# A convolution and SwiGLU layer on one core: the sixteen dot products of the first norm's gate move from the start of the second input stage to the end of the first

## The chip, the core and the metric

The kernel runs on one core of a Trainium2 chip. A core has TensorE (PE, matrix products into PSUM), VectorE (DVE), ScalarE (ACT), GpSimd (POOL) and SyncE (SP), which here only issues transfers. Each engine works off its own list of instructions in order and waits for the others by semaphores. The metric is the device time of one execution in microseconds; lower is better.

## What is computed

With DEPTH 1 the reference is one layer over 2048 tokens of 1024 features, float32, batch 1:

```python
c_act = jax.nn.silu(c)
mod = c_act @ ada_w[0] + ada_b[0]
sh_m, sc_m, g_m, sh_f, sc_f, g_f = jnp.split(mod, 6, axis=-1)
h = modulate(rms_norm(x, norm_gains[0, 0]), sh_m, sc_m)
h = short_conv_mixer(h, conv_w_in, conv_w, conv_w_out)   # 1024 -> 3072, gate_c * v,
                                                         # 3 taps, gate_b, 1024 -> 1024
x = x + g_m * rms_norm(h, norm_gains[0, 1])
h = modulate(rms_norm(x, norm_gains[0, 2]), sh_f, sc_f)
h = swiglu(h, w_gate_up, w_down)                         # 1024 -> 2 x 2816 -> 1024
x = x + g_f * rms_norm(h, norm_gains[0, 3])
```

The change is about `g_m`, the third of the six vectors of 1024 numbers that come from the conditioning vector `c`. In the kernel it is number 2 (numbered from 0). It is the gate by which the normalised result of the convolution mixer is scaled before it is added to `x`.

## The kernel before

**Stages.** The tokens are worked on in two units of 1024, each unit in two halves of 512 tokens. Every unit passes four stages of matrix products: `in` (the input projection with the convolution behind it), `out` (the output projection), `gu` (gate and up) and `down`. Their order is in0, out0, in1, out1, gu0, down0, gu1, down1. Tiles carry the stage's name: `in1P` is a block of PSUM in the second input stage.

**Products.** Each 2 x 2 product of blocks is made with seven products, P1 to P7, instead of eight, from sums and differences of blocks of the features (A11, A12, A22, S1 to S4) and of the weights. To keep float32 accuracy each operand is split into a high and a low part (`...h` and `...l`), and three matmuls stand for one product. One slot is one such product for one group of output columns: four blocks of 128 features, 12 matmuls of 128x512. The whole program is one list of slots, and slot numbers are the clock of the code: `first["in1"]` is the number of the slot with which in1 begins. in0 has 84 slots, out0 has 36, in1 has 84; the first two of out0 stand ahead of the last two of in0, so `first["out0"]` is 82 and `first["in1"]` is 120.

**Order.** For each slot the code first prepares weights for later slots (`supply`: load, sum, split into high and low), then does what was scheduled for this slot, then the small generators that are due (`due`), then the matmuls (`multiply`) and what follows on them. All engines keep the order in which the code issues, so an instruction that is issued early and waits holds up what stands behind it on the same engine. `schedule(slot, f)` runs `f` at a slot; a generator that yields a number goes on that many slots later.

**The modulation vectors.** Vectors 0 and 1 are made at the very start. The others, one each, are made by `mods_later(ms, pace)`: for each half of `c` it loads the row of `c`, spread over all partitions, applies Silu on ACT, and then makes eight dot products on VectorE (`tensor_tensor_reduce`, in the trace CUSTOM_DVE_ANT_0 with a short DVE_READ_ACCUMULATOR2_ANT behind it), each over a tile of 128 rows by 512 columns of `ada`, that is 16 for a vector. Each tile of `ada` is loaded by SP three steps ahead of its product. After the 16 products three small operations form the result, for vector 2 `mG[0]`. Between two steps lie `pace` slots. Vector 3 is scheduled at `first["out0"] - 2`, vector 4 at `first["in1"] + 60`, vector 5 in down0.

**Who uses it.** `mG[0]` is read by `after_out`, which starts when a half of `out0` is done and begins its own scaling about 40 slots later, inside in1.

**Tiles that are shared.** The tiles of `ada` and of the row of `c` come from the pool `raw`: 16 tiles of 128x512. From the same pool come the weight blocks of the input stage (`in10b`), the weights for the sums of the output stage (`out3b`), the rows of `x` for the next unit's norm (`xr`), the output stage's weights, and in in0 one of the PSUM copies of each group (`self.c22`, made by ACT). A load whose tile is not free yet waits on SP, and all of SP's later loads and stores wait behind it. Split weights use a pool of seven pairs (`wp`).

**Around the places.** In the last slots of in0 run the last weight sums for the output stage (`sums_later("out", ...)` from slot 24, on POOL and SP) and the norm of the next unit's rows (`norm_of_rows`, from slots 51 and 77, on ACT and SP). At the beginning of in1 `normalized` prepares the features of the new unit: it scales the loaded tiles a to d on VectorE, shifts them on ACT, and makes the seven operands (`s1`, `s3`, `s4`, `upper`, `lower`, `high`, `low`). In1's first groups read their weights from DRAM, where in0 left them (`in5P2k` is such a load).

Of the kernel before, what the change touches and what calls it, by code (L numbers as in the profile page):

```python
# [49 lines left out]
def hybrid_conv_layer(  # L50
# [43 lines left out]
    def raw(name):  # L94
        return raws.tile([P, CH], F32, tag="raw", bufs=NRAW, name=name)
# [7 lines left out]
    def small(n, name):  # L103
        return sb.tile([P, n], F32, tag="small", bufs=16, name=name)
# [8 lines left out]
    def later(slots, f):  # L113
        waiting.append((now[0] + slots, len(waiting), f))

    def run(gen):


        def step():
            n = next(gen, None)  # L120
            if n is not None:
                later(n, step)

        step()
# [38 lines left out]
    def col(t, k):  # L163
        return t[:, k : k + 1]
# [8 lines left out]
    def mods_later(ms, pace):  # L173

        s2 = {(m, h): sb.tile([P, KD], F32, tag="ms", bufs=4, name=f"ms{m}_{h}") for m in ms for h in range(2)}
        for h in range(2):
            half = slice(h * CH, (h + 1) * CH)
            row = raw(f"c{ms[0]}_{h}")
            SP.dma_start(row, c_row[:, half].to_broadcast((P, CH)))
            todo = [(m, n) for m in ms for n in range(KD)]  # L180
            tiles = {}

            def load(i, half=half, todo=todo, tiles=tiles):
                if i < len(todo):
                    m, n = todo[i]
                    tiles[i] = raw(f"ada{m}_{half.start}_{n}")
                    SP.dma_start(tiles[i], ada[m - 1, n][:, half])

            load(0)
            yield pace  # L190
            load(1)
            yield pace
            A.activation(row, row, AF.Silu)
            load(2)
            yield pace
            for i, (m, n) in enumerate(todo):
                load(i + 3)
                t = tiles.pop(i)
                V.tensor_tensor_reduce(t, t, row, 1.0, 0.0, ALU.mult, ALU.add, col(s2[m, h], n))
                yield pace  # L200
        for m in ms:
            i, which = m // 3, m % 3
            t = small(KD, f"mf{m}")
            V.tensor_tensor(t, s2[m, 0], s2[m, 1], ALU.add)
            b = vt[:, VB + m * KD : VB + (m + 1) * KD]
            if which == 0:
                V.tensor_tensor(mB[i], t, b, ALU.add)
            else:
                V.tensor_tensor(t, t, b, ALU.add)
                g = VG + (2 * i + which - 1) * KD  # L210
                if which == 1:
                    V.scalar_tensor_tensor(mA[i], t, 1.0, vt[:, g : g + KD], ALU.add, ALU.mult)
                else:
                    V.tensor_tensor(mG[i], t, vt[:, g : g + KD], ALU.mult)
            yield 1
# [650 lines left out]
    slots, first, own = [], {}, {}  # L866
# [13 lines left out]
    def schedule(slot, f):  # L880
        events.setdefault(max(slot, 0), []).append(f)
# [503 lines left out]
    schedule(24, lambda: run(sums_later("out", range(4), 2)))  # L1385
    schedule(first["gu0"] + 64, lambda: run(sums_later("down", range(12), 1.1)))
    schedule(first["out0"] - 2, lambda: run(mods_later((3,), 1.25)))
    schedule(first["in1"] - 8, lambda: run(mods_later((2,), 1.25)))
    schedule(first["in1"] + 60, lambda: run(mods_later((4,), 1.25)))
    schedule(first["down0"] + 22, lambda: run(mods_later((5,), 2)))  # L1390
    schedule(first["down1"] + 73, lambda: before_last(phases[-1]))
# [92 lines left out]
```

## Time and profile before

| | |
|---|---|
| median of 3 runs | 1970.31 us (1970.17 to 1972.41) |
| the profiled execution | 1969.02 us |
| its span, from first to last instruction | 1967.2 us |
| busy: PE, DVE, ACT, POOL | 1939.6, 1464.8, 870.2, 342.4 us |
| transferred | 459.51 MB, mean 234 GB/s |
| granted TensorE clock | 1.000 of full speed |

All durations below come from the profiled execution. In a timeline row stand the start, the length, the engine, the line of the code (always L78, the helper through which all instructions pass), the operation, the tiles as out<-in, the shape, the count and, in brackets, how long the engine was idle before it and whose signal came last. In a list of waits stand the total, how often, and the longest. SPq is SP's queue of transfers. Where a wait for several signals ended, the name given is the one that came last by the profile, which need not be the one that mattered.

### The profile page before, as it was taken

The page shows a single profiled execution, that of the slowest core. Times are in us where ns is not written, and L with a number is a line of the kernel's source. Part 1 is how long each engine was busy: PE and PEld are TensorE (multiplying, and loading weights), DVE is VectorE, ACT ScalarE, POOL GpSimd, SP SyncE. Part 2 cuts the span into 40 slices and gives each one's busy share as a digit, 9 for nine tenths or more (in the row PEclk, how much of TensorE's full clock was granted, in tenths as well). Part 3 has the DMA queues.
Part 4 walks back from the last instruction along what each step waited for, and adds up shares of the span by engine and source line. Part 5 has one row for each costly group of instructions (what it writes and reads, how often), then busy time and mean ns, then how long its engine had stood idle before and what let it go on. Part 6 is the DMA issues. An engine that isn't in the chain of part 4 may idle for free.

```text
span 1967.2 us, 24986 instructions
## 1 busy us (share of the span) xinstructions
PE 1939.6 (99%) x8468; PEld 1571.7 (80%) x8468; DVE 1464.8 (74%) x2159; ACT 870.2 (44%) x1430; POOL 342.4 (17%) x224
## 2 busy tenths in 40 slices
PE   8899999999999999999999999999999999999998
PEld 4578887777888888888888888888888888888886
DVE  5998888988998876997776755586776655665466
ACT  4533447534335643444333454463333333444452
POOL 0012202201221301243341410120100100111010
PEclk9999999999999999999999999999999999999999
DMA  9369859869996764677665977577554342386534
GB/s 390 137 230 390 306 178 350 314 236 373 327 319 228 265 228 146 223 240 249 212 211 189 307 292 264 181 278 270 195 194 136 126 142 97 118 312 232 196 133 133
DMA packets 204752, 459.51 MB, mean 234 GB/s; under 512 B 22864, under 2 KB 38352, under 8 KB 198224
## 3 DMA queue, kind: packets, MB, share of 16 engines
q1 hardware_dynamic: 180000, 403.52, 59.4%
q10 hardware_dynamic: 24624, 54.40, 7.2%
q8 instruction: 66, 1.08, 0.2%
q14 instruction: 62, 0.51, 0.1%
HBM read 326.75 MB, written 131.07 MB: 233 GB/s over the span
## 4 chain that ended last, share of the span: by engine, by line
PE 88%; DVE 5%; DMA 3%; issue 2%; ACT 1%; SPq 0%; POOL 0%; ACTq 0%; POOLq 0%; DVEq 0%
PE gu0P L78 21%; PE gu1P L78 21%; PE in0P L78 11%; PE down0P L78 11%; PE down1P L78 9%; PE in1P L78 8%; PE out1P L78 4%; PE out0P L78 2%; DVE in1c L78 0%; DVE ada L78 0%; DMA in0a<-xt_d 0%; DMA c<-c_row_d 0%; DMA y1S<-in1b1s 0%; DVE in1y L78 0%; PE pms L78 0%
## 5 line engine op out<-in xcount | busy, mean ns | idle before, releaser
L78 DVE TENSOR_TENSOR gu1a<-gu1P,gu1a 128x512 f32<-128x512 f32 x63 | 43.5, 691 | 108.6 <-PE gu1P L78 108.6
L78 DVE TENSOR_TENSOR gu0a<-gu0P,gu0a 128x512 f32<-128x512 f32 x63 | 43.3, 688 | 70.2 <-PE gu0P L78 68.6
L78 POOL TENSOR_TENSOR gu1a<-gu1a 128x512 f32<-128x512 f32 x11 | 19.0, 1726 | 363.5 <-DVE gu1g11s L78 42.5
L78 ACT COPY gu1a<-gu1P 128x512 f32<-128x512 f32 x42 | 24.7, 587 | 98.6 <-PE gu1P L78 87.4
L78 POOL TENSOR_TENSOR nq<-nq,nq 128x512 f32<-128x512 f32 x28 | 41.6, 1485 | 129.4 <-ACT nq L78 99.4
L78 ACT COPY gu0a<-gu0P 128x512 f32<-128x512 f32 x42 | 24.4, 586 | 83.8 <-PE gu0P L78 82.7
L78 DVE CUSTOM_DVE_ANT_0 ada<-ada,c 128x512 f32<-128x512 f32 x80 | 57.8, 733 | 0.0
L78 ACT COPY gu1g<-gu1P 128x512 f32<-128x512 f32 x24 | 14.1, 588 | 92.9 <-PE gu1P L78 92.9
L78 POOL TENSOR_TENSOR gu0a<-gu0a 128x512 f32<-128x512 f32 x11 | 19.4, 1767 | 171.4 <-ACT gu0a L78 48.0
L78 POOL TENSOR_TENSOR down0q<-down0q,down0q 128x512 f32<-128x512 f32 x14 | 23.8, 1703 | 144.1 <-ACT down0q L78 144.1
L78 ACT COPY gu0g<-gu0P 128x512 f32<-128x512 f32 x24 | 14.1, 587 | 75.9 <-PE gu0P L78 75.4
L78 POOL TENSOR_TENSOR down1q<-down1q,down1q 128x512 f32<-128x512 f32 x10 | 16.1, 1612 | 148.6 <-ACT down1q L78 148.6
L78 DVE TENSOR_TENSOR gu1g<-gu1P,gu1g 128x512 f32<-128x512 f32 x24 | 16.6, 691 | 27.4 <-ACT gu1g L78 26.0
L78 ACT ACTIVATE gu1a<-gu1a 128x512 f32<-128x512 f32 x42 | 26.6, 633 | 13.2 <-DVE xo L78 6.0
L78 DVE TENSOR_TENSOR down2P<-down2P,down2P 128x512 fp32r<-128x512 f32 x14 | 11.1, 794 | 28.6 <-ACT down2P L78 28.6
L78 ACT ACTIVATE gu0a<-gu0a 128x512 f32<-128x512 f32 x42 | 26.6, 633 | 11.7 <-DVE gu0a L78 10.4
L78 POOL TENSOR_TENSOR out1q<-out1q,out1q 128x512 f32<-128x512 f32 x14 | 22.3, 1594 | 51.2 <-ACT out1q L78 51.1
L78 POOL TENSOR_TENSOR out0q<-out0q,out0q 128x512 f32<-128x512 f32 x14 | 23.0, 1641 | 44.6 <-ACT out0q L78 44.5
L78 DVE TENSOR_TENSOR xx<-xx,zz 128x512 f32<-128x512 f32 x32 | 27.1, 847 | 1.1
L78 ACT ACTIVATE nq<-xx 128x512 f32<-128x512 f32 x32 | 20.2, 631 | 17.3 <-DVE xx L78 17.3
L78 DVE TENSOR_TENSOR gu0g<-gu0P,gu0g 128x512 f32<-128x512 f32 x24 | 16.5, 689 | 14.7 <-ACT gu0g L78 13.3
L78 DVE TENSOR_TENSOR down10P<-down10P,down10P 128x384 fp32r<-128x384 f32 x14 | 8.6, 615 | 22.3 <-ACT down10P L78 22.3
(3225 smaller groups left out, 6729.3 us busy)
## 6 DMA issues: line engine op xcount, KB each, us to landing
ada<-ada_d SPq DMA_DIRECT2D x64, 256.0 KB, 5.6
act0A<-gu0a SPq DMA_DIRECT2D x33, 256.0 KB, 3.5
act1A<-gu1a SPq DMA_DIRECT2D x33, 256.0 KB, 2.8
ada<-ada_d SPq DMA_DIRECT2D x16, 512.0 KB, 9.4
zz<-z SPq DMA_DIRECT2D x32, 256.0 KB, 5.2
xx<-xt_d SPq DMA_DIRECT2D x32, 256.0 KB, 5.5
x<-xx ACTq DMA_DIRECT2D x32, 256.0 KB, 4.9
down0S<-act0S SPq DMA_DIRECT2D x8, 1024.0 KB, 7.1
```

The costliest lines, as they stand in the source:

```text
L78: return tc.keep_in_program_order(f(*args, **kwargs))
```

## The change

One line. The generator for vector 2 starts 23 slots before out0, that is at slot 59, with one slot between its steps; before, it started eight slots before in1, at slot 112, with 1.25 slots between them.

```diff
     schedule(first["out0"] - 2, lambda: run(mods_later((3,), 1.25)))
-    schedule(first["in1"] - 8, lambda: run(mods_later((2,), 1.25)))
+    schedule(first["out0"] - 23, lambda: run(mods_later((2,), 1.0)))
     schedule(first["in1"] + 60, lambda: run(mods_later((4,), 1.25)))
```

By the generator's steps (three, eight products, three, eight products) it takes 22 slots and then forms the result: slots 59 to 81 after the change, 112 to 139.5 before. It issues 18 loads on SP (two rows of `c`, sixteen tiles of `ada`), two Silu on ACT, and sixteen products and the three small operations on VectorE, the same in both kernels. Vector 3 keeps its slot 80, so it now follows vector 2 instead of going ahead of it.

## The prediction

> **What bounds the kernel now.** I read the page first (span, busy times, transfers), then the list of waits of TensorE by stretch, then the timelines of the engines around each wait, then the busy times by stretch.
>
> ```profile
> span 1967.2 us, 24986 instructions
> PE 1939.6 (99%) x8468; PEld 1571.7 (80%) x8468; DVE 1464.8 (74%) x2159; ACT 870.2 (44%) x1430; POOL 342.4 (17%) x224
> ada<-ada_d SPq DMA_DIRECT2D x64, 256.0 KB, 5.6
> ```
>
> TensorE is the bound: 99% busy. So the change can only win where TensorE waits, or lose by making it wait. The list of TensorE's waits has nothing between 466 and 1900 us. In the stretch that holds the beginning of the second input stage (360 to 466 us) it has this:
>
> ```profile
> PE in1P L78 <- ACT in1c L78: 2.1, 2, 1.2
> PE in1P L78 <- DVE n00q L78: 0.9, 1, 0.9
> PE in1P L78 <- DVE in1S2l L78: 0.6, 1, 0.6
> PE in1P L78 <- DVE in1C L78: 0.4, 1, 0.4
> PE in1P L78 <- DVE in1c L78: 0.2, 1, 0.2
> PE in1P L78 <- DMA in6P3k<-kin6P: 0.2, 1, 0.2
> ```
>
> That is 4.4 us of waiting, seven waits. Four of them stand in its timeline here (those on in1S2l, in1C and DVE's in1c lie between 374.71 and 397.89); the first two rows give TensorE's pace:
>
> ```profile
> 360.02 0.61 PE L78 MATMUL in1P<-in1A11h,in3P1k 128*128 128x512 f32 x2
> 362.74 0.61 PE L78 MATMUL in1P<-in1A11h,in4P1k 128*128 128x512 f32 x2
> ...
> 374.71 0.70 PE L78 MATMUL in1P<-in1A12h,in5P2k 128*128 128x512 f32 x2 [0.93 <-DVE n00q L78]
> 397.89 0.50 PE L78 MATMUL in1P<-in1S1h,in3P5k 128*128 128x512 f32 x1 [0.82 <-ACT in1c L78]
> 434.83 0.73 PE L78 MATMUL in1P<-in1S1h,in0P 128*128 128x512 f32 x2 [1.24 <-ACT in1c L78]
> 463.39 0.70 PE L78 MATMUL in1P<-in1S4h,in6P3k 128*128 128x512 f32 x2 [0.19 <-DMA in6P3k<-kin6P]
> ```
>
> A slot (12 matmuls) takes 362.74 - 360.02 = 2.72 us. Twelve slots lie between 360.02 and the product in1S1h,in3P5k. Without waiting it would begin at 360.02 + 32.6 = 392.7 (less than a microsecond later with a norm's eight one-column matmuls in between, which I leave out); it begins at 397.89. So up to 5.2 us are lost there, more than the waits listed (4.4 less those of 434.83 and 463.39, about 3), because the matmuls just after a wait run slow too.
>
> **What holds TensorE there.** VectorE works almost without a gap from 362 to 396 us, and the moved products stand in its row. Of its timeline and ACT's:
>
> ```profile
> 366.99 0.68 DVE L78 CUSTOM_DVE_ANT_0 ada<-ada,c 128x512 f32<-128x512 f32 x1
> 367.67 1.27 DVE L78 TENSOR_TENSOR out0z<-out0P,out0z 128x512 f32<-128x512 f32 x2
> 368.87 0.67 DVE L78 CUSTOM_DVE_ANT_0 ada<-ada,c 128x512 f32<-128x512 f32 x1
> 369.72 4.43 DVE L78 TENSOR_TENSOR in1e<-in1a,in1c 128x512 f32<-128x512 f32 x4 [0.17 <-ACT in1c L78]
> 375.74 0.68 DVE L78 CUSTOM_DVE_ANT_0 ada<-ada,c 128x512 f32<-128x512 f32 x1
> 381.42 2.28 DVE L78 TENSOR_TENSOR in1c<-in1c,in1d 128x2048 f32<-128x2048 f32 x1
> 389.05 0.68 DVE L78 CUSTOM_DVE_ANT_0 ada<-ada,c 128x512 f32<-128x512 f32 x1
> 389.65 1.29 DVE L78 TENSOR_TENSOR in1S2l<-in1a,in1S2h 128x512 fp32r<-128x512 f32 x2
> 393.13 2.28 DVE L78 TENSOR_TENSOR in1b<-in1b,in1a 128x2048 f32<-128x2048 f32 x1
> ...
> 368.98 2.55 ACT L78 ACTIVATE in1c<-in1c,mB 128x512 f32<-128x512 f32 x4
> 378.34 2.71 ACT L78 ACTIVATE in1d<-in1d,mB 128x512 f32<-128x512 f32 x4 [2.07 <-DVE in1d L78]
> 395.45 1.91 ACT L78 CAST in1S4h<-in1b 128x2048 fp32r<-128x2048 f32 x1 [5.66 <-DVE in1b L78]
> 397.26 0.58 ACT L78 COPY in1c<-in1P 128x512 f32<-128x512 f32 x1
> 433.67 0.62 ACT L78 CAST in0P<-in0b 128x512 fp32r<-128x512 f32 x1 [1.57 <-PE in1P L78]
> ```
>
> Read it from the end: TensorE waits at 397.89 for ACT's copy of in1P (397.26), which stands behind the cast in1S4h (395.45), which waited 5.66 us for VectorE's in1b (393.13). Ahead of that VectorE runs unbroken back to 369.72. One product takes 389.65 - 389.05 = 0.60 us of its time. Four stand between 369.72 and 393.13, the first at 375.74 and the last at 389.05.
>
> The first wait, at 374.71, is put down to n00q, but the weights in5P2k are what came last. Their load stood in SP's queue behind a moved load:
>
> ```profile
> 368.74 0.82 SPq L78 DMA_DIRECT2D ada<-ada_d  x1
> 369.67 0.37 SPq L78 DMA_DIRECT2D in5P2k<-kin5P  x1
> ```
>
> **The change part by part.** Removed from the second input stage: 16 products on VectorE (16 x 0.60 = 9.6 us), the small sums behind them, two Silu on ACT, 16 loads of ada and two of the c row on SP's queue. Up to 397.89:
>
> 1. The product at 366.99 goes, so out0z (367.67) comes 0.6 us earlier. ACT squares it before it shifts in1c (368.98), and in1e (369.72) waits for that shift. So in1e starts 0.6 us earlier. The product at 368.87 wins nothing: the 0.17 us of idle time shows that in1e waited for ACT.
> 2. The one at 375.74 goes: another 0.6, 1.2 so far. ACT's shift of in1d moves along with it.
> 3. The next one stands just ahead of in1c + in1d (381.42). That sum needs ACT's last shift, which ends at 378.34 + 2.71 = 381.05, so only about 0.3 of its 0.6 us is won: 1.5.
> 4. The other two (the last at 389.05) lie in an unbroken row: 1.2 more, 2.7 at in1b.
> 5. Cast and copy on ACT follow, and TensorE's product comes at 395.2 instead of 397.89. That is later than 392.7, so nothing else needs to be faster than now. The waits before it shrink or vanish inside this sum; in5P2k, needed at 374.71 - 0.93 = 373.8, leaves the queue at least 0.9 us earlier (369.67 - 368.74), with out0z's store ahead of it 0.6 earlier: 1.5 us, more than the wait.
>
> Gain there: 2.7 us. Bounds: 0.9 (only the wait for in5P2k goes, something not seen holds in1b) and 5.2 (all that is lost). I take 2.7, because each step has its row.
>
> After that: the wait of 1.24 us at 434.83 stays. The copy there stands behind the cast of 433.67, which waited for TensorE itself (for a weight buffer). The wait of 0.19 at 463.39 goes, 0.3 us with the slow matmul after it: VectorE is rid of the eight products of the second half as well, and the loads ahead of in6P3k follow its stores. Nobody else waits until 1900 us, so what is won stays: 2.7 + 0.3 = 3.0 us.
>
> Added, ahead of the first output stage. Slot first["out0"] is where out0P begins, at 273.62, and 23 slots earlier (23 x 2.72 = 62.6) is 211 us. By the code the 16 products come one a slot, with three slots of loads ahead of each half: they end by 274.
>
> ```profile
> 273.62 0.62 PE L78 MATMUL out0P<-out0A110h,out0P 128*128 128x512 f32 x2
> ...
> 126.00:211.00 85.00, 85.00 (x376) 70.36 (x375) 75.44 (x108) 31.31 (x56) 23.95 (x15) 1.00 0.99 374
> 211.00:274.00 63.00, 63.00 (x277) 51.79 (x277) 47.23 (x80) 25.76 (x52) 9.45 (x7) 1.00 0.68 230
> 337.00:443.00 106.00, 101.86 (x451) 82.55 (x450) 96.93 (x160) 50.18 (x79) 20.53 (x12) 1.00 0.79 276
> 443.00:466.00 23.00, 22.81 (x100) 18.22 (x98) 18.30 (x32) 10.12 (x18) 1.29 (x1) 1.00 1.02 363
> ```
>
> Columns of the last four rows: length, busy time of PE, PEld, DVE, ACT, POOL, granted clock, DMA share, GB/s. At the new place VectorE has 47.23 of 63 us; with 9.6 and the small sums it is 57.3, 91%. The 18 transfers of 256 KB are 4.7 MB, 75 GB/s more: 305. The stretch just before ran at 75.44 of 85 us (89%), a DMA share of 0.99 and 374 GB/s, and TensorE was busy 85.00 of 85.00. So I price the new place at 0, covered by VectorE's 15.8 us of idle time; if that cover fails, the price is the last rival's. SP's queue there gets the 18 issues, with w_in, w_out and x rows behind them; ACT, with 25.76 of 63 us, takes the two Silu. The gate is first read here, so an earlier result is not waited for and wins nothing:
>
> ```profile
> 458.93 0.75 DVE L78 SCALAR_TENSOR_TENSOR zz<-zz,mG,n00r 128x512 f32<-128x512 f32 x1
> ```
>
> **The sum.** The profiled execution took 1969.02 us, 1.8 beside its span; less 3.0 it is 1966.0. The median of the runs is 1.3 above it (1970.31), so I predict 1967.3.
>
> **The rivals.** *More is won.* The four in1e take 4.43 us where two such operations of the same size take 1.29 (389.65), so 2.6 undisturbed; they collide with POOL. If the shift by 0.6 us ends the collision, 1.8 us more come off the row, and the gain is 2.7 + 1.8 + 0.3 = 4.8 us, still within the 5.2: 1965.5. Against it: POOL's sums there are released through ACT by out0z, which moves as well. Chance 0.2.
> [...]
>
> *Nothing is won.* The DMA engines become the bound behind it: in6P3k lands when it lands now, and TensorE, 2.7 us ahead, waits 2.7 longer at 463.39. For it: the DMA share is 1.02 just there (443 to 466). Against it: the transfers ahead are stores of VectorE's results and loads into freed buffers, which move along. 1970.3, chance 0.17.
>
> *It is slower.* The tiles of the moved loads come out of the ring of 16 "raw" tiles that also serves the w_in blocks, the x rows, the sums for w_out and the copies of a product block. By the code five more are held in slots 62 to 66, and SP already waits there for tiles to come free:
>
> ```profile
> SPq L78 <- DMA kout2P<-out2b: 4.5, 3, 3.0
> ...
> 215.79 0.59 ACT L78 COPY in0b<-in0P 128x512 f32<-128x512 f32 x1 [3.46 <-PE in0P L78]
> 221.03 0.61 PE L78 MATMUL in0P<-in0S4h,in8P 128*128 128x512 f32 x2
> ```
>
> That copy takes such a tile, and in0S4h,in8P may begin only when it is done: 221.03 - 216.38 = 4.65 us of slack. If a tile comes three slots late (8.2 us), TensorE loses 3.5. Two such copies fall into the full slots: 7.0 less 3.0 is 4.0 slower, 1974.3. It decides from a delay of 4.65 + 1.5 = 6.2 us on both. Against it: VectorE's and ACT's release of tiles follows TensorE slot by slot, and I count a delay of one to two slots. Chance 0.11.
>
> **How the numbers follow.** The forecast has 0.52, with 1966.4 to 1969.1 as its own range (2.7 replaced by 3.6, halfway to the first rival, or by the bound of 0.9). The range reaches to the first two rivals: down to 1964.8 (the bound of 5.2 and the 0.3) and up to 1971.2 (nothing won, and a part of the slower case); it leaves out most of the slower case and a little of each end. Measurement tells about 0.2% (3.9 us) from no change. Faster by more than that: the rival that wins 4.8, 0.2, and a little of the forecast, 0.22. Slower: 0.11. Within: 0.67.
>
> **What would show it.** Right, if in the new profile: TensorE's wait at in5P2k is gone; in1b ends some 2.7 us earlier against the start of in1P; the wait on ACT in1c behind in1S4h is shorter but there; one wait of 1.2 us on ACT in1c remains in the product in1S1h,in0P; no wait of TensorE appears between 210 and 274 us, with VectorE near 91%. Wrong, if TensorE waits for ACT in0b or in0c there (the ring), if in6P3k is waited for by 2 us or more, or if in1e's four take under 3 us.

## The result

| | median | |
|---|---|---|
| before | 1971.13 us | 1968.90 to 1972.41, 16 runs |
| after | 1967.57 us | 1965.52 to 1969.67, 16 runs |
| after / before | 0.9981 | 95% interval 0.9975 to 0.9988 |

The change wins 3.6 us, 0.19%. The same kernel timed again beside the last experiments gave 1967.09 against 1970.43, a ratio of 0.9983 (0.9974 to 0.9991), 3.3 us. Predicted were 3.0 us and 1967.3. The profiled execution took 1968.11 us, only 0.9 less than the one before (1969.02); where the rest of the gain went in this execution is told below.

### The profile page after: what moved, and what is told of

It reads as the page before. It is cut to its first block, busy times and chain, and to the rows that moved or that the text cites. A ratio compares the mean times of both kernels' runs of the same rounds, so it can differ in the third digit from the quotient of the medians.

```text
span 1966.3 us, 24998 instructions
## 1 busy us (share of the span) xinstructions
PE 1939.7 (99%) x8468; PEld 1572.9 (80%) x8468; DVE 1463.6 (74%) x2159; ACT 870.3 (44%) x1430; POOL 343.1 (17%) x224
## 4 chain that ended last, share of the span: by engine, by line
PE 92%; DVE 3%; issue 2%; DMA 2%; ACT 1%; POOL 0%; ACTq 0%; POOLq 0%; SPq 0%; DVEq 0%
PE gu0P L78 21%; PE gu1P L78 21%; PE in0P L78 11%; PE down0P L78 11%; PE in1P L78 10%; PE down1P L78 9%; PE out1P L78 4%; PE out0P L78 3%; DMA x<-xx 0%; DMA in0a<-xt_d 0%; DMA c<-c_row_d 0%; PE pms L78 0%; DVE down1z L78 0%; DVE in1y L78 0%; DMA in7P2k<-kin7P 0%
## 5 line engine op out<-in xcount | busy, mean ns | idle before, releaser
L78 ACT COPY gu1a<-gu1P 128x512 f32<-128x512 f32 x42 | 24.7, 588 | 98.5 <-PE gu1P L78 87.4
```

The lines of the kernel that those rows point to most:

```text
L78: return tc.keep_in_program_order(f(*args, **kwargs))
```

## The profile after

The span, then the whole list of TensorE's waits from 360 to 1900 us (total, times, longest):

```profile
span 1966.3 us, 24998 instructions
```

```profile
PE in1P L78 <- ACT in1c L78: 2.3, 2, 1.4
PE in1P L78 <- DMA in7P2k<-kin7P: 0.4, 1, 0.4
```

Seven waits of 4.4 us before are three of 2.7 now. The timelines of TensorE, VectorE and ACT at the places that the prediction named:

```profile
361.49 0.61 PE L78 MATMUL in1P<-in1A11h,in3P1k 128*128 128x512 f32 x2
375.09 0.61 PE L78 MATMUL in1P<-in1A12h,in5P2k 128*128 128x512 f32 x2
396.62 0.73 PE L78 MATMUL in1P<-in1S1h,in3P5k 128*128 128x512 f32 x2 [0.84 <-ACT in1c L78]
...
370.79 3.15 DVE L78 TENSOR_TENSOR in1e<-in1a,in1c 128x512 f32<-128x512 f32 x4 [0.78 <-ACT in1c L78]
373.87 1.25 DVE L78 TENSOR_TENSOR n00t<-n00p 128x4 f32<-128x4 f32 x1
381.37 2.29 DVE L78 TENSOR_TENSOR in1c<-in1c,in1d 128x2048 f32<-128x2048 f32 x1 [0.19 <-ACT in1d L78]
391.86 2.28 DVE L78 TENSOR_TENSOR in1b<-in1b,in1a 128x2048 f32<-128x2048 f32 x1
...
394.18 1.91 ACT L78 CAST in1S4h<-in1b 128x2048 fp32r<-128x2048 f32 x1 [5.05 <-DVE in1b L78]
395.99 0.57 ACT L78 COPY in1c<-in1P 128x512 f32<-128x512 f32 x1
```

Counted from the first matmul of in1P (360.02 before, 361.49 after), in1b begins at 30.37 instead of 33.11 us, and in3P5k at 35.13 instead of 37.87: 2.74 us earlier, both. The wait at in5P2k is gone; the one behind the cast in1S4h is still there.

One wait is new: 0.4 us for in7P2k, in the slot that begins at 478.81. The lead over the kernel before, counted from the first matmul of in1P, is 3.2 us ahead of it and 2.5 behind it. The second execution of the changed kernel that was profiled (after_again) does not have this wait and keeps 3.6 us to the end. So "nobody else waits" held in one of the two.

The new place (211 to 274 us) and the stretch around in6P3k, columns as in the prediction; then, at the new place, ACT's two copies into raw tiles, VectorE's last piece of work for out0, and the product that reads it:

```profile
211.00:274.00 63.00, 63.00 (x278) 51.79 (x277) 57.89 (x111) 27.91 (x55) 10.65 (x7) 1.00 0.90 305
443.00:466.00 23.00, 23.00 (x103) 19.03 (x102) 17.07 (x30) 9.73 (x17) 0.00 (x0) 1.00 1.03 350
```

```profile
217.57 0.59 ACT L78 COPY in0b<-in0P 128x512 f32<-128x512 f32 x1 [3.47 <-DMA kout2P<-out2b]
238.21 0.59 ACT L78 COPY in0c<-in0P 128x512 f32<-128x512 f32 x1 [5.32 <-DVE in0y L78]
270.96 1.75 DVE L78 TENSOR_TENSOR out0A<-out0A,out0A110h 128x1536 fp32r<-128x1536 f32 x1
275.55 0.39 PE L78 MATMUL out0P<-out0A,out0P 128*128 128x512 f32 x1
```

TensorE is busy 63.00 of 63.00 us there: the products cost nothing at the new place. The copy at 217.57, though, no longer waits for TensorE but for a transfer that frees a tile.

## The experiments

All stretches are counted from the first matmul of in1P to the first matmul of the named product, and to the end of the span; they come from each kernel's timeline of TensorE. in6P3k stands for the product in1S4h,in6P3k. Ratios are to the kernel before, timed beside each, with the 95% interval.

| kernel | in1S1h,in3P5k | in1S1h,in0P | in6P3k | in1S2h,in1P | end | ratio |
|---|---|---|---|---|---|---|
| before | 37.87 | 74.81 | 103.37 | 106.21 | 1607.21 | 1 |
| after | 35.13 | 72.21 | 100.45 | 103.17 | 1604.81 | 0.9981 (0.9975 to 0.9988) |
| after_again | 34.95 | 71.82 | 100.05 | 102.77 | 1603.64 | 0.9983 (0.9974 to 0.9991) |
| e1_loads_stay | 34.73 | 73.12 | 104.19 | 106.91 | 1609.11 | 1.0003 (0.9994 to 1.0012) |
| e2_products_stay | 37.59 | 74.48 | 102.91 | 105.73 | 1606.56 | 0.9998 (0.9990 to 1.0007) |
| e3_first_half | 35.35 | 72.27 | 101.18 | 104.00 | 1605.52 | 0.9987 (0.9979 to 0.9996) |
| e4_second_half | 37.91 | 74.70 | 102.96 | 105.70 | 1606.68 | 1.0003 (0.9994 to 1.0012) |
| e10_loads_stay_weight_first | 35.01 | 70.51 | 100.89 | 105.30 | 1606.16 | 0.9991 (0.9982 to 1.0000) |
| e5_copy_first | 33.98 | 70.89 | 99.11 | 101.83 | 1603.83 | 0.9982 (0.9973 to 0.9991) |
| e6_weight_first | 34.99 | 70.50 | 99.57 | 102.44 | 1603.41 | 0.9987 (0.9978 to 0.9996) |
| e7_both | 33.69 | 69.05 | 98.63 | 101.51 | 1602.52 | 0.9978 (0.9970 to 0.9987) |

### Products or loads?

**e2_products_stay.** The changed kernel, with sixteen unread products at the old place and no loads of `ada` there:

```diff
     schedule(first["out0"] - 23, lambda: run(mods_later((2,), 1.0)))
+    schedule(first["in1"] - 8, lambda: run(products_only(1.25)))
```

> The changed kernel, and sixteen products of the same size are made on VectorE in the old place by the old timetable, on two tiles loaded once; their result is not used. No load of ada stands there. Theory (VectorE's row): the stretch from the first in1P to in1S1h,in3P5k returns to 37.5 to 37.9 us, the time to within 0.5 us of before (in5P2k, whose wait was SP's, may still win a little, but the later waits take it up). Rival (the loads): 35.1, 3 us under before.

The ratio is 0.9998: the products alone take the gain back. The waits from 360 to 470 us are again those of before, except that those for in5P2k and in6P3k are missing without the loads:

```profile
PE in1P L78 <- ACT in1c L78: 2.7, 2, 1.5
PE in1P L78 <- DVE in1S2l L78: 0.6, 1, 0.6
PE in1P L78 <- DVE in1c L78: 0.5, 1, 0.5
PE in1P L78 <- DVE in1C L78: 0.4, 1, 0.4
```

**e1_loads_stay.** The counterpart: products early, and at the old place 18 loads that nothing reads.

```diff
     schedule(first["out0"] - 23, lambda: run(mods_later((2,), 1.0)))
+    schedule(first["in1"] - 8, lambda: run(loads_only(2, 1.25)))
```

> The changed kernel, and the 18 loads of the old place (two rows of c, sixteen tiles of ada) are issued there as well, by the old timetable; nothing reads them, and no product is made there. Measured from the first in1P matmul to the first matmul of in1S1h,in3P5k the kernel before has 37.87 us and the changed one 35.13. Theory (VectorE's row ahead of in1b is what was shortened): 35.1 to 35.4, a wait of up to 0.3 us may return at in5P2k, and the time stays some 3 us under before. Rival (the loads in SP's queue and on the DMA engines were what held in1): 37 to 38, and the time of before.

In the first 35 us the expectation held: in3P5k comes at 34.73, although in5P2k is waited for again (0.8 us). But the ratio is 1.0003. What was won is lost at in1S1h,in0P, of which the rows of TensorE, ACT and SP's queue say this, and below them the stretch before and the stretch behind (columns as above, the third last is the granted clock):

```profile
433.18 1.22 PE L78 MATMUL in1P<-in1S1h,in0P 128*128 128x512 f32 x2 [2.73 <-ACT in1c L78]
438.46 1.01 PE L78 MATMUL in1P<-in1A11h,in6P1k 128*128 128x512 f32 x2
...
432.02 0.62 ACT L78 CAST in0P<-in0b 128x512 fp32r<-128x512 f32 x1 [3.59 <-DMA kgu0P<-gu0P]
432.54 0.58 ACT L78 COPY in1c<-in1P 128x512 f32<-128x512 f32 x1
...
426.54 0.40 SPq L78 DMA_DIRECT2D kgu0P<-gu0P  x1
```

```profile
426.00:432.40 6.40, 4.44 (x20) 3.36 (x18) 6.33 (x11) 1.00 (x2) 0.00 (x0) 1.00 0.87 246
432.40:439.30 6.90, 6.12 (x14) 4.79 (x15) 4.31 (x10) 1.92 (x4) 3.45 (x2) 0.51 0.63 229
```

ACT's cast needs a pair buffer, which here comes free when a store issued at 426.54 has landed; the copy that TensorE needs stands behind the cast. The wait is 2.73 us instead of 1.24, and for the next 6.9 us TensorE has half its clock: its slot lasts 5.28 us (433.18 to 438.46) instead of 2.72. So 1.5 + 2.6 us are lost, more than the 3.1 won before.

**e10_loads_stay_weight_first.** To see whether that buffer is the cause: e1 with two neighbours exchanged in the order of weights, so that the weight in0P3 (in0P in ACT's row above) takes the pair that gu0P7 had.

```diff
+    a = next(i for i, w in enumerate(order) if w.key == ("gu", 0, "P7") and w.keep)
+    order[a], order[a + 1] = order[a + 1], order[a]
+    position[position.index(a + 1)] = a
```

> The kernel whose products are made early while 18 unread loads stay at the old place (1.0003 of the kernel before), now with the weight in0P3 ahead of gu0P7. Theory (what it lost against the changed kernel, some 4.5 us, is the wait of 2.73 us at in1S1h,in0P for a pair buffer whose store comes late, with the 6.8 us at half clock behind it): that wait and the half clock go, and the time is 3 to 4 us under the kernel before (0.9980 to 0.9985). Rival (the loads themselves cost that much, by the DMA engines' time or SP's queue): another wait as long takes its place, for in6P3k or a weight before it, and the time stays within 1 us of the kernel before.

Both were half right. The wait at in1S1h,in0P is gone, and about 2.4 us with it (0.9991 against 1.0003, though the two intervals just overlap). But it is not down to 0.998, because the loads make a later weight late:

```profile
PE in1P L78 <- DMA in6P3k<-kin6P: 2.1, 1, 2.1
PE in1P L78 <- ACT in1c L78: 0.7, 1, 0.7
PE in1P L78 <- DMA in5P2k<-kin5P: 0.4, 1, 0.4
```

```profile
462.90:466.30 3.40, 3.40 (x10) 2.62 (x9) 3.37 (x6) 1.63 (x3) 0.00 (x0) 0.50 1.04 411
```

The DMA engines are full there (share 1.04, 411 GB/s), and this wait too is followed by 3.4 us at half clock. So either part, left at the old place, is enough to lose the gain (0.9998 and 1.0003), by separate ways: the products through VectorE's order, the loads through weights and buffers that come late. How much the loads cost depends on what stands around them. e10 differs from e6 below by the unread loads alone: it reaches in1S2h,in1P 2.9 us later (105.30 against 102.44), while the ratios of the times, 0.9991 and 0.9987, cannot be told apart.

### Which half of the products?

**e3_first_half** and **e4_second_half** move only one half of the group to the new place; the other stays where it was. The edit is an order and a pause in the generator:

```diff
-    schedule(first["out0"] - 23, lambda: run(mods_later((2,), 1.0)))
+    schedule(first["out0"] - 23, lambda: run(mods_later((2,), 1.0, (0, 1), 55.75, 1.25)))   # e3
+    schedule(first["out0"] - 23, lambda: run(mods_later((2,), 1.0, (1, 0), 42, 1.25)))      # e4
```

> Only the first half of the row (one load of c, eight tiles, eight products) is made early; the second half keeps its old slots (from 125.75, pace 1.25), behind in1S1h,in3P5k but for one product. Theory: that stretch stays at 35.1 to 35.4 us; what returns is the wait at in6P3k (0.3 us), so 2.5 to 3 us under before. Rival (the gain is spread evenly over the sixteen products): half of it, 1.5 us under before.

> Only the second half of the row is made early; the first half's eight products and loads keep their old slots (112 to 123, pace 1.25). Theory: the stretch to in1S1h,in3P5k is that of before, 37.5 to 37.9 us; only the wait at in6P3k goes, so 0 to 0.6 us under before. Rival (spread evenly): 1.5 us under before.

As expected: the first half brings in3P5k to 35.35 us and the ratio to 0.9987; the second brings in3P5k nothing (37.91) and the time nothing (1.0003). What the second half adds once the first is gone is the wait for in6P3k, which is back in e3 (0.5 us). By the ratio alone e3 can't be told from the changed kernel; the stretches tell them apart.

### What covers the new place?

**e8_products_twice** makes each product twice there (the second sum is not read), **e9_loads_twice** adds 18 loads that nothing reads, **e11_loads_half_more** the nine of the first half.

```diff
                 V.tensor_tensor_reduce(t, t, row, 1.0, 0.0, ALU.mult, ALU.add, col(s2[m, h], n))
+                if ms == (2,):                                                            # e8
+                    V.tensor_tensor_reduce(t, t, row, 1.0, 0.0, ALU.mult, ALU.add, col(again, n))
...
+    schedule(first["out0"] - 23, lambda: run(loads_only(2, 1.0)))                           # e9, e11
```

> The changed kernel, with each of the sixteen products made twice at the new place (the second sum is not read): 16 x 0.6 = 9.6 us more of VectorE's time between 211 and 274 us, where it was busy 57.9 of 63. Theory of the prediction (the new place costs nothing because VectorE's idle time there, 15.8 us before and 5.1 after, covers it): 9.6 us are 4.5 more than what is left, so TensorE waits there and the time is 2 to 4.5 us above the changed kernel's. Rival (what covers it is not the idle time of the stretch but the slots by which VectorE may run behind TensorE): no new wait of TensorE from 211 to 300, and the changed kernel's time within 1 us.

> The changed kernel, with 18 more loads of 256 KB at the new place that nothing reads (16 blocks of ada and two rows of c): 4.7 MB more between 211 and 274 us, where 305 GB/s were moved with a DMA share of 0.90, and twice as many of the 16 raw tiles taken. Theory (the new place is covered; 380 GB/s are no more than the 374 that the stretch from 126 to 211 moved with TensorE never waiting): no more than 1 us above the changed kernel. Rival (the ring of 16 raw tiles decides, the slower case of the prediction with its margin used up): ACT's copies in0b and in0c come late, TensorE waits for them, and the time is 4 to 8 us above the changed kernel's, above that of the kernel before.

> The changed kernel with 9 more unread loads at the new place (first half only) instead of 18, which cost 12 us by two waits of 3.8 and 3.9 us for ACT's copies in0b and in0c. Theory (each half of the loads makes one copy late, by holding raw tiles): the first wait, for in0b ahead of in0S4h,in8P, is there with 3 us or more, the second is under 1 us, and the time is 5 to 7 us above the changed kernel's. Rival (the ring has room for nine more loads but not for eighteen): no wait of 1 us there and the time within 1 us of the changed kernel's.

| | median | ratio |
|---|---|---|
| e8_products_twice | 1978.45 us | 1.0040 (1.0027 to 1.0053) |
| e9_loads_twice | 1979.22 us | 1.0042 (1.0028 to 1.0055) |
| e11_loads_half_more | 1978.15 us | 1.0035 (1.0023 to 1.0047) |

All three are 10 to 12 us slower than the changed kernel, more than e8's theory (2 to 4.5 us) and e9's rival (4 to 8) had said. e8's rival, e9's theory and e11's rival were wrong, and e11's theory had only the first wait right. in1 begins at 373.31, 372.97 and 372.50 us instead of 361.49. (Ahead of the new place's first product TensorE is 1.03 us later in e8 than in the changed kernel; in e9, but for its wait of 3.76 us there, it would begin in0S4h,in8P at 220.96 us instead of 222.50. The last section says where such steps come from.) Of the changed kernel and of e8 the row that places TensorE, and of e8 VectorE's out0A and the product that waits for it; then of e11 TensorE's, ACT's and SP's rows:

```profile
222.50 0.62 PE L78 MATMUL in0P<-in0S4h,in8P 128*128 128x512 f32 x2
```

```profile
223.53 0.61 PE L78 MATMUL in0P<-in0S4h,in8P 128*128 128x512 f32 x2
...
282.66 1.75 DVE L78 TENSOR_TENSOR out0A<-out0A,out0A110h 128x1536 fp32r<-128x1536 f32 x1
284.47 0.80 PE L78 MATMUL out0P<-out0A,out0P 128*128 128x512 f32 x1 [4.05 <-DVE out0A L78]
```

```profile
226.15 0.95 PE L78 MATMUL in0P<-in0S4h,in8P 128*128 128x512 f32 x2 [3.43 <-ACT in0b L78]
250.28 1.15 PE L78 MATMUL in0P<-in0S4h,in9P 128*128 128x512 f32 x2 [3.17 <-ACT in0c L78]
...
225.52 0.58 ACT L78 COPY in0b<-in0P 128x512 f32<-128x512 f32 x1 [9.98 <-DMA dada<-ada_d]
...
220.31 0.38 SPq L78 DMA_DIRECT2D dada<-ada_d  x1
```

In e8, out0A comes 11.7 us later than in the changed kernel (282.66 against 270.96). 1.0 of that is there before the products begin (223.53 against 222.50, and already 215.37 against 214.34 at in0S1h,in8P); the other 10.7 us are nearly all that the fifteen products added ahead of out0A take (0.73 us from the start of a product to that of its repeat, 15 x 0.73 = 11.0). Yet VectorE was busy only 57.5 of 63 us up to 274: what idle time it has there is spent waiting for others in its order, and can't be used. In e11, ACT's copy begins (225.52) as soon as an unread load has landed whose tile it takes (issued at 220.31, 5.1 us to landing). That is the prediction's slower rival, at the copies in0b and in0c that it named; my expectation that nine loads would hit only the first copy was wrong (they run from slot 59 to 70 and reach both). Each wait of over 3 us is again followed by half clock: granted 0.50 from 283.2 to 290 us in e8 and from 224.8 to 228.2 in e9, and in e11 pairs of matmuls of 1.06 and 1.05 us behind the two waits, instead of 0.62.

### What is left?

**e5_copy_first** puts the cast in1S4h one slot later on ACT; **e6_weight_first** is the exchange of e10 on the changed kernel; **e7_both** has both.

```diff
-            ("P3", -8, f.s4), ("P3", -6, partial(f.high, "S4")), ("P3", -5, partial(f.low, "S4")),
+            ("P3", -8, f.s4), ("P3", -6 + (f.ph.kind == "in"), partial(f.high, "S4")), ("P3", -5, partial(f.low, "S4")),
```

> The changed kernel, with the cast in1S4h put one slot later in ACT's order, so that ACT's copy of in1P (in1c) stands ahead of it. Theory (what is left of the wait at in1S1h,in3P5k, 0.84 us, is the copy standing behind the cast, which waits for VectorE's in1b): the wait goes, from the first matmul of in1P to in3P5k it takes about 34.3 us instead of 35.13, and the time is 0.8 to 1.0 us under the changed kernel's (0.9981 of the kernel before), so about 4.4 under the kernel before. Rival (TensorE would wait there for something else that comes just as late, such as VectorE's in1C or in1S1l): the stretch stays at 35.1 and the time at the changed kernel's. Rival (the later cast makes in1S4h late for in3P3k three slots on): a new wait of up to 1 us there, no gain.

> The changed kernel, with the weight in0P3 ahead of gu0P7 in the order in which the pair buffers are given out and ACT casts. Theory (the wait at in1S1h,in0P, 1.24 us before and 1.42 after, is ACT's cast of that weight waiting for a pair buffer, with the copy in1c behind it): in0P3 gets the buffer that gu0P7 had, is cast about 3 us earlier, the wait there goes, and the time is 1.4 to 1.7 us under the changed kernel's (0.9981 of the kernel before), so about 5 under the kernel before. Rival (gu0P7, now later, and the transfers behind it make the next weight late): the wait moves to the next weights (in6P6k, in6P7k or in0P4) and nothing is won.

> The changed kernel once more, for comparison with the two kernels that build on it. Expected at 0.9981 of the kernel before (0.9975 to 0.9988). Its profile may differ by one thing: whether a stretch of 3.4 us at a granted clock of 0.5 falls into the first 90 us, which costs 1.5 to 1.7 us.

> The changed kernel with both reorderings: the cast in1S4h one slot later on ACT, and the weight in0P3 ahead of gu0P7. Theory (the two waits, at in1S1h,in3P5k and at in1S1h,in0P, are independent of each other): both are gone, the product in1S2h,in1P begins about 101.2 us after the first matmul of in1P instead of 103.17, and the time is about 2 us under the changed kernel's, 0.9970 to 0.9975 of the kernel before. Rival (the DMA engines are what is late next: in6P3k was waited for by 0.8 us when the second wait alone went, and it lands when it lands): the wait there grows to 1.9 us, and the time is only 0.8 to 1 us under the changed kernel's.

Of e5 (ACT, TensorE), of e6 (ACT, TensorE), and the one wait from 360 to 1900 us that e7 has:

```profile
390.08 0.59 ACT L78 COPY in1c<-in1P 128x512 f32<-128x512 f32 x1 [1.23 <-PE in1P L78]
393.90 1.91 ACT L78 CAST in1S4h<-in1b 128x2048 fp32r<-128x2048 f32 x1 [3.22 <-DVE in1b L78]
...
395.32 0.62 PE L78 MATMUL in1P<-in1S1h,in3P5k 128*128 128x512 f32 x2
```

```profile
429.20 0.62 ACT L78 CAST in0P<-in0b 128x512 fp32r<-128x512 f32 x1 [2.14 <-PE in1P L78]
429.72 0.58 ACT L78 COPY in1c<-in1P 128x512 f32<-128x512 f32 x1
...
460.74 0.70 PE L78 MATMUL in1P<-in1S4h,in6P3k 128*128 128x512 f32 x2 [0.83 <-DMA in6P3k<-kin6P]
```

```profile
PE in1P L78 <- DMA in6P3k<-kin6P: 1.3, 1, 1.3
```

Each edit removes its wait (1.15 us of the stretch to in3P5k in e5; in e6 the copy runs at 429.72, before TensorE needs it), and the stretches add up. Then in6P3k becomes what is late, as e7's rival said. Of its issue (timeline of SP's queue) and the time to its landing (the last number of a row of the page's transfers, here from 440 to 470 us), first in the changed kernel, then in e7:

```profile
453.57 0.38 SPq L78 DMA_DIRECT2D in6P3k<-kin6P  x1
```

```profile
in6P3k<-kin6P SPq DMA_DIRECT2D x1, 512.0 KB, 7.3
```

```profile
449.11 0.51 SPq L78 DMA_DIRECT2D in6P3k<-kin6P  x1
```

```profile
in6P3k<-kin6P SPq DMA_DIRECT2D x1, 512.0 KB, 8.9
```

Issued 2.5 us earlier against the start of in1P (89.57 instead of 92.08), it lands only about 0.9 earlier (98.5 instead of 99.4). In time, e5 and e6 can't be told from the changed kernel. What e5 had won at in1S2h,in1P against the second execution of the changed kernel (101.83 against 102.77) is gone at the end (1603.83 against 1603.64): among others it waits 0.4 us for ACT's in1C at 562.17. e7 has the lowest median, 1966.13 against 1967.09 of the changed kernel beside it; of the 2 us expected about half shows, and the intervals of the two ratios overlap.

## Why the prediction was right

**VectorE's row.** Term by term, against the start of in1P: in1e began 0.4 us earlier (predicted 0.6), in1c + in1d 1.52 (1.5), in1b 2.74 (2.7), in3P5k 2.74 (2.7); then 0.30 more up to in1S2h,in1P (0.3), together 3.04 (3.0). The second execution has 3.44. e2, e3 and e4 show that it is the products of the first half, by VectorE's order. That the middle terms fit to 0.02 us is in part luck: in1e fell 0.2 short of its 0.6, and a collision that the sum had left out gave 0.2 back (next paragraph).

**The collision with POOL** (the rival by which more is won) half came and went. The four in1e took 3.15 us instead of 4.43, but the small n00t behind them took 1.25. Before the change that operation, and in both kernels POOL's, were:

```profile
374.08 0.15 DVE L78 TENSOR_TENSOR n00t<-n00p 128x4 f32<-128x4 f32 x1
372.19 1.42 POOL L78 TENSOR_TENSOR out0q<-out0q,out0q 128x512 f32<-128x512 f32 x1 [1.49 <-ACT out0q L78]
```

```profile
373.26 1.84 POOL L78 TENSOR_TENSOR out0q<-out0q,out0q 128x512 f32<-128x512 f32 x1 [1.67 <-ACT out0q L78]
```

1.28 us won in the one and 1.10 lost in the other: POOL's sum moved, for the most part, past the end of in1e and onto n00t, which ends at 375.12 as the sum does at 375.10. That the two collide is inferred from the single operations in the two traces: in1e's first operation before the change (369.72, 1.52 us) began while POOL's sum of 369.21 to 370.69 ran, its last (372.38, 1.78 us) during that of 372.19 to 373.61, its first after the change (370.79, 1.35 us) during that of 370.29 to 371.59; the other five took about 0.68 us each.

**The most that could be won** was put 1 us too high at 5.2, mostly by the norm's matmuls that it left out. In e7 the list shows no wait of TensorE between the first matmul of in1P and in3P5k, and the stretch is 33.69 us, so 37.87 - 33.69 = 4.2 us are lost before. The rival that wins 4.8 (4.5 of it here) would not have fitted.

**in5P2k** left the queue 1.27 us earlier (predicted 1.5, needed 0.9). **in6P3k** did not "land when it lands": it landed 3.9 us earlier against in1's start (issue and time to landing give 103.3 before and 99.4 after), which is why the rival "nothing is won" failed. A queue that is 18 loads lighter is not enough for that: in e2, without the loads but with the products, it landed at 102.8. With the products gone and the loads kept it was 102.1 (e1) and 100.8 (e10). That fits what the prediction had said against this rival, that the transfers ahead move along with the engines; it takes both parts to move it by 3.9 us, and no run splits that number cleanly. e7 shows how near the rival was: 1 us more and it binds.

**Where the account was incomplete.** The prediction put the gain down to the products and gave the moved loads only in5P2k and part of the 0.3 at in6P3k. e1 shows that the loads alone can cost as much: left at the old place they lengthen the wait at in1S1h,in0P, which the prediction had as "stays", and bring the half clock; with that wait out of the way (e10) they lengthen the one for in6P3k. The total was right because both went together. "Nobody else waits" was not quite right either: in the first profile the wait for in7P2k took 0.7 us of the 3.2 back.

**The new place** cost nothing, with VectorE at 57.89 us (57.3 predicted) and 305 GB/s (305). But the cover that I named, VectorE's idle time, was not the one that counts. What counts is how late the last link may be: out0A ended at 272.71, for a product at 275.55, so 2.8 us were left; ACT's copies, by their start against in1's, were delayed by 0.3 us (in0b) and 1.9 (in0c), and had about 4.3 and 2.7 left. The slower rival's price of 7.0 for delays of three slots was too low: e9 and e11 lost 10 to 12. The two waits themselves are near it (3.43 + 3.17 = 6.6 in e11); what it left out is the half clock behind each (211 to 274 us at a mean granted clock of 0.95 in e11 and 0.92 in e9, 1.00 in the changed kernel).

## What to carry to other kernels

Follow the wait back through each engine's order, and count only what stands in that row; then ask the same of the loads that move with it, since each of the two can be enough to lose the gain. At a new place, don't count idle time as cover: look for the first thing in the order that another engine needs, and how many microseconds it is early. When a wait goes, look at the next transfer on a full stretch of the DMA engines: it says how much more can be won.

## What the runs showed of the hardware

A wait of TensorE can cost more than its length: in e1 one that was 1.5 us longer cost 2.6 us more behind it. The granted clock in the profile falls to 0.50 right behind a wait, for 3.40 us (the changed kernel, e10) or about twice that (0.51 for 6.90 us in e1). Of the changed kernel, then of the one before, two stretches each, columns as above:

```profile
80.50:83.80 3.30, 1.63 (x7) 0.82 (x6) 3.30 (x6) 1.14 (x2) 0.00 (x0) 1.00 0.00 0
83.90:87.30 3.40, 3.40 (x10) 2.64 (x9) 3.37 (x7) 1.10 (x2) 0.00 (x0) 0.50 0.00 0
```

```profile
80.50:83.80 3.30, 1.62 (x6) 0.73 (x5) 3.30 (x6) 1.24 (x2) 0.00 (x0) 1.00 0.00 0
83.90:87.30 3.40, 3.40 (x16) 2.81 (x15) 3.37 (x7) 1.10 (x2) 0.00 (x0) 1.00 0.00 0
```

The two kernels do the same there, with the same two waits of 0.83 to 0.84 us that end at about 81.7 and 83.5, and TensorE was busy for half of the stretch that holds them (1.63 and 1.62 us of 3.30). In the changed kernel the next stretch ran at half clock, with 10 matmuls instead of 16; before, the clock stayed at 1.00. So neither these waits nor this busy share decide alone, and what does is not shown. The half clock is why in1 starts at 361.49 there and at 360.02 before. In all profiles that reach in1 by the same way its start falls into such steps: 359.5 to 360.1 us (before, e1, e2, e7), 361.1 to 361.6 (the changed kernel twice, e3, e5, e6, e10) and 362.40 (e4). That none, one and two stretches at half clock make these steps is shown by the rows above for the kernel before and the first profile of the changed one, and inferred for the others. With the 0.7 us lost at in7P2k it is why the profiled execution of the changed kernel shows 0.9 us of gain and the medians 3.6. It also limits what an edit of 1 us can show: 1.5 us come and go from run to run.

A single wait of 2.14 (e10), 2.73 (e1) or 3.43 us (e11) was followed by half clock each time; one of 1.48 us in in1 (e2, at 397.45, with pairs of matmuls of 0.62 to 0.63 us behind it) and one of 1.80 us in in0 (before, at 71.39, with a clock of 1.00 from 71.2 to 74.5) were not. Two waits of 0.83 and 0.84 us close together were once enough (the changed kernel) and once not (before).
